# Convolution inputs in a second buffer pool, two narrower operands, and the bias shifts placed one by one in a streaming-encoder layer

## The chip, the cores and the metric

The kernel runs on one core of a Trainium2 chip. The metric is the device time of one execution in microseconds (us), lower is better; a version's time is the median of several runs. One execution is also recorded by the hardware profiler, and all rows of a profile or trace below are from that one.

## The reference: what is computed

One layer of a causal encoder on an input `x` of 2048 tokens by 1024 features, in float32. The input is normalised, multiplied by one wide projection, and the columns of the result feed three groups of heads: chunked softmax attention with a learned bias by relative distance, an mLSTM with a short causal convolution on its queries and keys, and gated linear attention (GLA). The groups are concatenated, projected back and normalised. The parts that the change touches, cut from the reference:

```python
def causal_conv(x, w):                       # 4 taps along the sequence
    xp = jnp.pad(x, ((0, 0), (k_w - 1, 0), (0, 0)))
    return sum(xp[:, j:j + s] * w[j] for j in range(k_w))

z = jnp.einsum('bsd,de->bse', rmsnorm(x, norm_g), w_in)
(aq, ak, av, ag, mq, mk, mv, mo, mi, mf, mg, gq, gk, gv, ga, gg) = jnp.split(z, split_idx, axis=-1)
# attention: scores + bias[clip(relative distance)]; softmax; p @ v; times silu(ag)
qk = jax.nn.silu(causal_conv(jnp.concatenate([mq, mk], axis=-1), conv_w))
# mLSTM on qk, mv with gates mi, mf; times sigmoid(mo), head norm, silu(mg)
log_alpha = jax.nn.log_sigmoid(einsum(ga, w_alpha) + b_alpha) / 16
# GLA on gq, gk, gv with log_alpha; head norm; times silu(gg)
```

## The kernel before, in words

The sequence is cut into four quarters of 512 tokens, `q` = 0 to 3. A first part of the program (call it part A) goes through the quarters: for each it projects the quarter's normalised input onto all columns, and weaves the mLSTM and GLA recurrences in between. Its results go to DRAM. A second part (part B, from `L955` on) reads them back, does the attention and the output projection.

Every projection of 128 columns (`proj_g`, `L231` to `L242`) is 24 matmuls of 128x512: eight blocks of the contraction, each in three products, because both operands are split in a high and a low half. They accumulate in a PSUM bank with the tag `ip`, of which there are two. So a projection can start only when the result of the last but one has been copied out of its bank. That copy is done by ScalarE, mostly: `L547` for the convolution inputs, `L486` (a tanh) for the gate columns, `L513` to `L515` for the values in `evac0`.

**The order of the work.** TensorE's instructions are in the order in which the program issues them (`tc.manual_schedule` names TensorE alone); a small planner, `Flow`, with a hand-written cost per piece, says where the pieces of the recurrences come between the projections. The instructions of all other engines and the DMA issues on the SyncE (SP) queue are ordered by the framework when the program is built, from priorities (the program's order, with the evacuations raised by `AHEAD`) and a simulated timeline. Each engine then runs its list strictly in order: an instruction that waits holds up all behind it. Buffers are taken from pools by name: a tile `name="u", bufs=1` has one buffer, and its next user waits until all readers of the last one are done.

One quarter of part A runs: `proj_z` (GLA's q and k), `proj_v` (values, `proj_t`), `proj_gg`, then `proj_m`, then `proj_gm`, then `proj_a`.

- `proj_m` (`L540` to `L561`) makes six projections, `b` = 0 to 5, the queries and keys of the mLSTM. Each result is copied by ScalarE (`L547`) into `zb`, a tile `u` of 3 + 512 columns with one buffer. GpSimd puts the last three columns of the quarter before in front (`L551`) and saves this one's (`L552`); ScalarE makes the first tap (`L554`), VectorE the other three (`L556`), and a tanh (`L558`, into one of two tiles `e`) and a product (`L559`) finish the SiLU.
- `proj_gm` (`L563` to `L570`) makes six more, `mo0 mg0 mo1 mg1 mo2 mg2`; each is copied out by a tanh in `sig_tile`.
- `gates` is a chain on the few gate columns; its temporaries, and the diagonal matrix `dg` of `prep_x`, the row scale `rbs` and the gate columns `g1` of `prep`, come from a pool `gpool` of five buffers of 512 columns, through `g_tile`.
- `gsel` is a constant matrix: 128 columns that make the GLA decay, then 64 of which the rows 0 to 5 and 32 to 37 of the product are used (`L434` to `L438`).
- `Kt` (7 x 128 columns) holds seven scaled key operands of a GLA chunk; GpSimd writes their first 16 to 112 columns (`L831`), TensorE reads 64 columns of the first four and 128 of the others (`L839`).
- `bias_rel`, called once in the quarter `q` = 1 after `proj_m`, loads the bias table `bt` (128 x 6 x 256) and shifts each head's part by a constant with six ScalarE instructions (`L615`); GpSimd then masks a corner (`L616`). Only part B reads `bt` (`L1071`).

Of the kernel before, what the change touches and what calls it, by code (L numbers as in the profile page):

```python
# [8 lines left out]
FP32 = mybir.dt.float32  # L9
FR = mybir.dt.float32r  # L10
AF = mybir.ActivationFunctionType
# [5 lines left out]
P = 128  # L17
D = 1024
KT = D // P
QT = 512  # L20
# [81 lines left out]
def trunk_kernel(ctx: ExitStack, tc: tile.TileContext, xT, x, w_f, w_t, w_o, w_gates, norm_g, conv_w,  # L102
                 gate_sel, one_row, bias, ml_g, gla_g, final_g, out):
    nc = tc.nc
# [13 lines left out]
    bt = const.tile([P, AH, 256], FP32, name="bt")  # L118
# [24 lines left out]
    with ExitStack() as pa_:  # L143
# [18 lines left out]
        wg = one.tile([P, KT, 32], FP32, name="wg")  # L162
        nc.gpsimd.memset(wg, 0.0)
        onerow = one.tile([P, 1], FP32, name="onerow")
        gsel = one.tile([P, P + 64], FP32, name="gsel")
        zero6 = one.tile([P, 1], FP32, name="zero6")[G0:G0 + MH]
        nc.vector.memset(zero6, 0.0)
        mlg = one.tile([P, 3], FP32, name="mlg")
# [22 lines left out]
            for r in range(4):  # L191
                nc.vector.memset(hs4[32 * h:32 * h + 32, r, 4 * h + r:4 * h + r + 1], 1.0)
        glg = one.tile([P, 2], FP32, name="glg")
        Kt = one.tile([P, 7, P], FP32, name="Kt")
        nc.gpsimd.memset(Kt, 0.0)
        Qb = one.tile([P, 8, 4, 16], FP32, name="Qb")
        nc.gpsimd.memset(Qb, 0.0)
        NP = 4
# [2 lines left out]
        st = {"zb": None, "m": zero6, "S": None, "B": None}  # L201

        def g_tile(shape):
            return gpool.tile(shape, FP32, name="g")

        def load_consts():
            nc.sync.dma_start(cw, conv_w)
# [35 lines left out]
        def proj_f(name, X):  # L243
            out_ = []
            for _ in proj_g(name, X, out_, 4):
                flow.piece(12 * 0.227)
            return out_[0]
# [183 lines left out]
        def gates(q, g1, R):  # L431
            t0 = q * QT
            pb = bank("pw")
            nc.tensor.matmul(pb[0:64], gsel[:, P:P + 64], g1, start=True, stop=True)  # L434
            gi = g_tile([P, QT])[G0:G0 + MH]
            fm = g_tile([P, QT])[G0:G0 + MH]
            nc.vector.tensor_copy(gi, pb[32:32 + MH])
            nc.scalar.copy(fm, pb[0:MH])  # L438
            yield 0.9, 3.0
            pa = bank("pw")  # L440
            nc.tensor.matmul(pa, gsel[:, 0:P], g1, start=True, stop=True)
            ls = big.tile([P, QT], FP32, name="ls", bufs=1)
            log_sigmoid([(ls, pa, g_tile([P, QT])), (fm, fm, g_tile([P, QT])[G0:G0 + MH])])
            R["ls"] = ls
            mr = g_tile([P, QT])[G0:G0 + MH]
            nc.vector.tensor_tensor_scan(mr, fm, gi, st["m"], op0=ALU.add, op1=ALU.max)
            bc = g_tile([P, QT])[G0:G0 + MH]
            for c in range(NC):
                cs = slice(c * L, (c + 1) * L)
                nc.vector.tensor_tensor_scan(bc[:, cs], ones[G0:G0 + MH], fm[:, cs], 0.0, op0=ALU.mult, op1=ALU.add)  # L450
            c4 = lambda t: t.rearrange("p (c t) -> p c t", t=L)
            nm = bc
            gb_ = gi
            nc.vector.tensor_tensor(gb_, gi, bc, op=ALU.subtract)
            nc.scalar.copy(rows[0:MH], gb_)
            nc.scalar.activation(rows[64:64 + MH], mr, AF.Exp, scale=-1.0)
            nc.vector.tensor_tensor(nm, bc, mr, op=ALU.subtract)
            nc.sync.dma_start(nm_d[q], nm)
            nc.vector.tensor_tensor(c4(gb_), c4(gb_), c4(nm)[:, :, L - 1:L].broadcast_to([MH, NC, L]), op=ALU.add)
            nc.scalar.activation(rows[32:32 + MH], gb_, AF.Exp)  # L460
            iw = rows[G0:G0 + MH]
            nc.vector.tensor_tensor(iw[:, 0:L], nm[:, 0:L], st["m"].broadcast_to([MH, L]), op=ALU.add)
            nc.vector.tensor_tensor(c4(iw)[:, 1:NC], c4(nm)[:, 1:NC], c4(mr)[:, 0:NC - 1, L - 1:L].broadcast_to([MH, NC - 1, L]),
                                    op=ALU.add)
            nc.scalar.activation(iw, iw, AF.Exp)
            ml = big.tile([P, 1], FP32, name="ml")[G0:G0 + MH]
            nc.vector.tensor_copy(ml, mr[:, QT - 1:QT])
            st["m"] = ml
            il = iw.rearrange("p (c t) -> p c t", t=L)[:, :, L - 1]
            nc.sync.dma_start(il_d[q], il)  # L470
            iwl = big.tile([P, MH, NC], FP32, name="iwl")
            nc.sync.dma_start(iwl, il_d[q].partition_broadcast(P))
            yield 0.9, 22.0
            rt_ps = bank("pw")
            for c in range(NC):
                nc.tensor.transpose(out=rt_ps[:, c * P:(c + 1) * P], in_=rows[:, c * L:(c + 1) * L], identity=ident)
            rt = big.tile([P, NC, 4, MH], FP32, name="rt")
            nc.vector.tensor_copy(rt, rt_ps.rearrange("p (c r e) -> p c r e", c=NC, r=4)[:, :, :, 0:MH])
            R["rt"] = rt
            R["iwl"] = iwl  # L480
            yield 0.5, 1.0

        def sig_tile(ps):
            th = ev.tile([P, QT], FP32, name="e")
            with tc.high_priority(offset=AHEAD):
                nc.scalar.activation(th, ps, AF.Tanh, scale=0.5)  # L486
            return th

        def silu_tile(ps):
# [50 lines left out]
        def proj_m(X):  # L540
            qk = big.tile([P, 6, QT], FP32, name="qk", bufs=1)
            tail = big.tile([P, 6, 3], FP32, name="tail")
            for b in range(6):
                ps = proj_f(("mq" if b < 3 else "mk") + str(b % 3), X)
                zb = big.tile([P, 3 + QT], FP32, name="u", bufs=1)
                with tc.high_priority(offset=AHEAD):
                    nc.scalar.copy(zb[:, 3:], ps)  # L547
                if st["zb"] is None:
                    nc.gpsimd.memset(zb[:, 0:3], 0.0)
                else:  # L550
                    nc.gpsimd.tensor_copy(zb[:, 0:3], st["zb"][:, b, :])  # L551
                nc.gpsimd.tensor_copy(tail[:, b, :], zb[:, QT:QT + 3])  # L552
                acc = qk[:, b, :]
                nc.scalar.activation(acc, zb[:, 0:QT], AF.Copy, scale=cw[:, b, 0:1])  # L554
                for i in range(1, 4):
                    nc.vector.scalar_tensor_tensor(acc, zb[:, i:i + QT], cw[:, b, i:i + 1], acc, op0=ALU.mult, op1=ALU.add)  # L556
                th = ev.tile([P, QT], FP32, name="e")
                nc.scalar.activation(th, acc, AF.Tanh, scale=0.5)  # L558
                nc.vector.scalar_tensor_tensor(acc, th, 1.0, acc, op0=ALU.add, op1=ALU.mult)  # L559
            st["zb"] = tail  # L560
            return qk  # L561

        def proj_gm(X):  # L563
            gm = big.tile([P, 3, QT], FP32, name="gm", bufs=1)
            for a in range(3):
                th = sig_tile(proj_f(f"mo{a}", X))
                nc.gpsimd.tensor_scalar(th, th, 1.0, mlg[:, a:a + 1], op0=ALU.add, op1=ALU.mult)
                sl = silu_tile(proj_f(f"mg{a}", X))
                nc.gpsimd.tensor_tensor(gm[:, a, :], th, sl, op=ALU.mult)
            return gm  # L570

        def att_in(q, X, b, ps):
# [36 lines left out]
        def bias_rel():  # L609
            bc = big.tile([P, AH], FP32, name="sm")  # L610
            nc.sync.dma_start(bc, bias[:, :, 256])
            nc.scalar.activation(bc, bc, AF.Copy, scale=-1.0)
            nc.sync.dma_start(bt, bias[:, :, 0:256])
            for h in range(AH):
                nc.scalar.activation(bt[:, h, :], bt[:, h, :], AF.Identity, bias=bc[:, h:h + 1])  # L615
            nc.gpsimd.memset(bt[0:64, :, 192:256], NEG)  # L616

        def m_tile(shape):
            return big.tile(shape, FP32, name="m", bufs=3)
# [191 lines left out]
        def gla(q, vg, gg, G, held=None):  # L811
            for sub in range(2):
# [7 lines left out]
                for c in range(2):  # L820
# [7 lines left out]
                        r = slice(32 * h, 32 * h + 32)  # L828
                        nc.scalar.copy(Qb[r][:, :, h, :], b16(qt)[r, 8 * c:8 * c + 8, :])
                    for i in range(1, 8):  # L830
                        nc.gpsimd.tensor_tensor(Kt[:, i - 1, 0:16 * i].rearrange("p (b j) -> p b j", j=16), ko[:, c, 0:i, :],  # L831
                                                Dt[:, c, i, 1:1 + i].unsqueeze(2).broadcast_to([P, i, 16]), op=ALU.mult)
                    tb = bank("gb")
                    nc.tensor.transpose(out=tb[:, 0:P], in_=dr[:, cs], identity=ident)
# [1 line left out]
                    of_ps = bank("ga")  # L836
                    for i in range(1, 8):
                        w = 64 if i < 5 else P
                        nc.tensor.matmul(of_ps[0:w, 64 * i:64 * i + 64], Kt[:, i - 1, 0:w], Qb[:, i, :, :].rearrange("p h i -> p (h i)"),  # L839
                                         start=True, stop=True)  # L840
                    kdt = big.tile([P, P], FP32, name="kdt", bufs=1)
                    nc.scalar.copy(kdt, tb[:, P:2 * P])
# [61 lines left out]
        for q in range(NQ):  # L904
# [32 lines left out]
            qk = proj_m(X)  # L937
            dg = prep_x(q + 1)
            flow.need("gates")
            if q == 1:  # L940
                bias_rel()
            M = dict(R)
            flow.start("mlstm", mlstm(q, qk, vs, M))
            M["gm"] = proj_gm(X)
            R = {}
            flow.start("prep", prep(q + 1, R, dg))
            proj_a(q, X)
# [7 lines left out]
    with ExitStack() as pb_:  # L955
# [3 lines left out]
        one = early  # L959
# [311 lines left out]
def _layout(inputs):  # L1271
# [32 lines left out]
    o["w_gates"] = np.ascontiguousarray(cat("ga", "mi", "mf").reshape(KT, P, 28).transpose(1, 0, 2))  # L1304
    o["norm_g"] = np.ascontiguousarray(a["norm_g"][0].reshape(KT, P).T)
    o["conv_w"] = np.ascontiguousarray(a["conv_w"][0].reshape(4, 6, P).transpose(2, 1, 0))
    gs = np.zeros((4, 32, P + 64), np.float32)
    gs[:, 0:16, 0:P] = a["w_alpha"][0]
    for h in range(MH):
        gs[:, 22 + h, P + 3 * (h % 2) + h // 2] = 1.0  # L1310
# [1 line left out]
    gs[0, 28, 0:P] = a["b_alpha"][0]  # L1312
    gs[0, 28, P:P + MH] = a["b_gates"][0][MH:][[0, 2, 4, 1, 3, 5]]
    gs[0, 28, P + 32:P + 32 + MH] = a["b_gates"][0][:MH][[0, 2, 4, 1, 3, 5]]
    gs = gs.reshape(P, P + 64)
    o["one_row"] = np.zeros((P, 1), np.float32)
    o["one_row"][28] = 1.0
    o["gate_sel"] = gs
# [27 lines left out]
```

## Time and profile before

| | |
|---|---|
| runs | 1284.54, 1284.47, 1280.35 us; median 1284.47 us |
| the profiled execution, device time | 1278.8 us |
| its span, first to last instruction | 1276.9 us |
| outside the span | 1.9 us |
| instructions | TensorE 6804 matmuls, VectorE 1869, ScalarE 1097, GpSimd 761 |
| mean granted TensorE clock | 0.990 |

How to read the rows: PE is a matmul on TensorE, PEld its weight load, DVE is VectorE, ACT is ScalarE, POOL is GpSimd, SP is SyncE, which issues DMAs. `L547` is line 547 of the kernel. A row of a timeline has the start, the duration, the engine, the line, the operation, what it writes and reads, how many were merged, and in brackets how long the engine had been idle and what ended that. A row of a list of waits has who waited for whom, the total in us, how often, and the longest. A row of a table by stretch has the stretch, its length, the busy time of PE, PEld, DVE, ACT and POOL with the count of instructions, the granted clock, the DMA share and GB/s. A row for one line or tile has the durations in ns as lowest/median/highest and the first and last start. Matmuls overlap: the duration of one is longer than the distance from its start to the next one's start.

### The profile page before, as it was taken

The numbers are of one execution on the slowest core, as the hardware profiler recorded it, in microseconds if no ns is written. First come the engines' busy times: TensorE is split into PE (matmuls) and PEld (weight loads), VectorE is DVE, ScalarE is ACT, GpSimd is POOL, SyncE is SP. The second block draws the span as 40 slices with busy tenths as digits, with TensorE's granted clock in tenths as the row PEclk, the third lists the DMA queues.
The fourth block names the chain that finished last, engine by engine and source line by source line (L and its number), as shares of the span: only waits on it lengthen the run. The fifth ranks groups of instructions, "written<-read, shape, count | busy, mean of one in ns | idle before, by whom it ended". The sixth has DMA issues, their size and how long they took to land.

```text
span 1276.9 us, 19361 instructions
## 1 busy us (share of the span) xinstructions
PE 1243.8 (97%) x6804; PEld 1008.3 (79%) x6804; DVE 813.7 (64%) x1869; ACT 590.1 (46%) x1097; POOL 592.2 (46%) x761
## 2 busy tenths in 40 slices
PE   9999999999999999999999999999989999999997
PEld 7777777778777788877778877887867888878886
DVE  6647736772675878266577766675577677666641
ACT  5635432562533346254333643332576565655631
POOL 3336663233666232276622446642364454454442
PEclk7999999999999999999999999999999999999999
DMA  7157344324733442472344233526886456555122
GB/s 246 27 158 259 111 124 150 118 73 131 258 96 114 143 129 66 136 260 88 108 138 124 84 127 98 138 72 175 282 258 205 156 181 207 165 184 172 50 83 82
DMA packets 100185, 184.31 MB, mean 144 GB/s; under 512 B 10592, under 2 KB 46304, under 8 KB 100088
## 3 DMA queue, kind: packets, MB, share of 16 engines
q1 hardware_dynamic: 95624, 174.95, 43.6%
q10 hardware_dynamic: 4464, 8.13, 1.7%
q8 instruction: 53, 0.87, 0.3%
q14 instruction: 44, 0.36, 0.1%
HBM read 147.35 MB, written 35.70 MB: 143 GB/s over the span
## 4 chain that ended last, share of the span: by engine, by line
PE 77%; DVE 8%; POOL 4%; DMA 4%; issue 3%; ACT 3%; SPq 0%; POOLq 0%; DVEq 0%; ACTq 0%
PE ip L236 11%; PE ip L238 10%; PE ip L237 10%; PE ip L256 4%; PE ip L1196 4%; PE ip L1198 4%; PE ip L1197 4%; PE ip L258 4%; PE ip L257 4%; PE s L1055 4%; PE tp L1115 3%; DVE qk L556 2%; PE w L1134 2%; PE ga L839 2%; PE w L1131 2%
## 5 line engine op out<-in xcount | busy, mean ns | idle before, releaser
L236 PE MATMUL ip<-x,w 128*128 128x512 f32 x784 | 318.8, 407 | 3.0 <-ACT u L547 2.7
L238 PE MATMUL ip<-x,w 128*128 128x512 f32 x784 | 306.4, 391 | 0.0
L237 PE MATMUL ip<-x,w 128*128 128x512 f32 x784 | 306.0, 390 | 0.0
L236 PEld LDWEIGHTS ip<-x,w 128*128 128x128 f32 x784 | 147.3, 188 | 46.8 <-issue 12.5
L238 PEld LDWEIGHTS ip<-x,w 128*128 128x128 f32 x784 | 147.2, 188 | 32.4
L237 PEld LDWEIGHTS ip<-x,w 128*128 128x128 f32 x784 | 147.5, 188 | 28.1 <-issue 1.4
L227 ACT CAST w<-wraw 128x1024 fp32r<-128x1024 f32 x126 | 131.7, 1046 | 31.4 <-PE ip L258 10.3
L228 POOL TENSOR_TENSOR w<-wraw,w 128x1024 fp32r<-128x1024 f32 x42 | 100.8, 2401 | 97.0 <-ACT w L227 97.0
L228 DVE TENSOR_TENSOR w<-wraw,w 128x1024 fp32r<-128x1024 f32 x84 | 114.6, 1366 | 45.5 <-ACT w L227 45.4
L1076 POOL TENSOR_SCALAR pt<-pt,sm 128x640 f32<-128x640 f32 (+2 forms) x96 | 72.2, 754 | 118.9 <-DVE sm L1075 92.5
L256 PE MATMUL ip<-w,x 128*128 128x512 f32 x256 | 102.2, 399 | 4.4 <-DVE e L492 2.9
L258 PE MATMUL ip<-w,x 128*128 128x512 f32 x256 | 99.8, 390 | 0.0
L257 PE MATMUL ip<-w,x 128*128 128x512 f32 x256 | 99.7, 390 | 0.0
L781 POOL TENSOR_TENSOR prd<-gk,zg 128x16 f32<-128x16 f32 (+7 forms) x112 | 67.1, 599 | 68.0 <-PE pw L787 62.0
L1074 ACT ACTIVATE pt<-pt,sm 128x640 f32<-128x640 f32 (+2 forms) x96 | 73.3, 763 | 48.3 <-DVE sm L1071 43.9
L1122 DVE TENSOR_TENSOR pl<-tp,ph 128x512 fp32r<-128x512 f32 (+1 forms) x108 | 71.9, 672 | 35.0 <-ACT ph L1121 34.8
L1055 PE MATMUL s<-kk,qq 128*128 128x256 f32 (+2 forms) x360 | 82.4, 314 | 2.3 <-DVE sm L1071 2.2
L778 POOL TENSOR_TENSOR gk<-gk,al 128x16 f32<-128x16 f32 (+14 forms) x120 | 69.6, 580 | 22.1 <-ACT al L755 14.6
L1121 ACT CAST ph<-tp 128x512 fp32r<-128x512 f32 (+1 forms) x108 | 60.3, 572 | 39.7 <-PE tp L1115 37.3
L486 ACT ACTIVATE e<-ip 128x512 f32<-128x512 f32 x44 | 26.2, 595 | 107.5 <-PE ip L238 91.5
L1055 PEld LDWEIGHTS s<-kk,qq 128*128 128x128 f32 x360 | 62.8, 190 | 16.1 <-DVE sm L1071 5.8
L556 DVE SCALAR_TENSOR_TENSOR qk<-u,cw,qk 128x512 f32<-128x512 f32 x72 | 65.7, 913 | 13.7 <-ACT qk L554 12.2
(342 smaller groups left out, 2483.4 us busy)
## 6 DMA issues: line engine op xcount, KB each, us to landing
wraw<-in_w_f SPq DMA_DIRECT2D x100, 512.0 KB, 3.6
wraw<-in_w_t SPq DMA_DIRECT2D x28, 512.0 KB, 3.6
qq<-q_d SPq DMA_DIRECT2D x48, 256.0 KB, 4.8
kk<-k_d SPq DMA_DIRECT2D x18, 512.0 KB, 6.5
vv<-v_d SPq DMA_DIRECT2D x18, 512.0 KB, 5.8
xraw<-in_xT SPq DMA_DIRECT2D x16, 512.0 KB, 8.5
xr<-in_x SPq DMA_DIRECT2D x16, 512.0 KB, 3.7
out<-xr ACTq DMA_DIRECT2D x31, 256.0 KB, 2.2
```

The costliest lines, as they stand in the source:

```text
L227: nc.scalar.copy(w[:, :, 0, :], rv)
L228: other().tensor_tensor(w[:, :, 1, :], rv, f32(w[:, :, 0, :]), op=ALU.subtract)
L236: nc.tensor.matmul(ps, w[:, k, 0, :], X[k][:, 0, :], start=(k == 0), stop=False)
L237: nc.tensor.matmul(ps, w[:, k, 0, :], X[k][:, 1, :], start=False, stop=False)
L238: nc.tensor.matmul(ps, w[:, k, 1, :], X[k][:, 0, :], start=False, stop=(k == KT - 1))
L256: nc.tensor.matmul(ps, X[k][:, 0, t], w[:, 0, :], start=(k == 0), stop=False)
L257: nc.tensor.matmul(ps, X[k][:, 0, t], w[:, 1, :], start=False, stop=False)
L258: nc.tensor.matmul(ps, X[k][:, 1, t], w[:, 0, :], start=False, stop=(k == KT - 1))
L556: nc.vector.scalar_tensor_tensor(acc, zb[:, i:i + QT], cw[:, b, i:i + 1], acc, op0=ALU.mult, op1=ALU.add)
L1055: nc.tensor.matmul(sp[:, :cn], qq[:, l, tt * P:(tt + 1) * P], kk[:, ko + c0:ko + c0 + cn], start=(l == 0), stop=(l == 1))
L1074: nc.scalar.activation(pt[:, :n], pt[:, :n], AF.Exp, bias=init, scale=-1.0, accum_out=sm[:, 2:3])
L1076: nc.gpsimd.tensor_scalar(pt[:, :n], pt[:, :n], sm[:, 3:4], 0.5, op0=ALU.mult, op1=ALU.mult)
```

## The change

Four edits.

1. `g_tile` makes every buffer of `gpool` three columns wider and hands out its first 512 columns. In `proj_m` the odd inputs (`b` = 1, 3, 5) take their `zb` from `gpool`; the even ones stay in the single `u`.
2. `gsel` loses its last 16 columns, 64 becomes 48.
3. `Kt` becomes two tiles: four operands of 64 columns and three of 128.
4. `bias_rel` becomes a generator. Its loads stay where they were; each of the six shifts is issued in `proj_gm` of the quarter 1 after one of the six tanhs, and tied behind that tanh in ScalarE's list with `tc.issue_after`; the mask follows the last.

```diff
-        gsel = one.tile([P, P + 64], FP32, name="gsel")
+        gsel = one.tile([P, P + 48], FP32, name="gsel")
...
-        Kt = one.tile([P, 7, P], FP32, name="Kt")
-        nc.gpsimd.memset(Kt, 0.0)
+        Kh = one.tile([P, 4, 64], FP32, name="Kh")
+        nc.gpsimd.memset(Kh, 0.0)
+        Kl = one.tile([P, 3, P], FP32, name="Kt")
+        nc.gpsimd.memset(Kl, 0.0)
+        Kt = [Kh[:, i] for i in range(4)] + [Kl[:, i] for i in range(3)]
...
         def g_tile(shape):
-            return gpool.tile(shape, FP32, name="g")
+            t = gpool.tile([P, 3 + QT], FP32, name="g")[:, 0:QT]
+            return t.rearrange("p (c t) -> p c t", c=shape[1]) if len(shape) > 2 else t
...
-            nc.tensor.matmul(pb[0:64], gsel[:, P:P + 64], g1, start=True, stop=True)
+            nc.tensor.matmul(pb[0:48], gsel[:, P:P + 48], g1, start=True, stop=True)
...
-                nc.scalar.activation(th, ps, AF.Tanh, scale=0.5)
+                st["th"] = nc.scalar.activation(th, ps, AF.Tanh, scale=0.5).ins
...
-                zb = big.tile([P, 3 + QT], FP32, name="u", bufs=1)
+                zb = gpool.tile([P, 3 + QT], FP32, name="g") if b % 2 else big.tile([P, 3 + QT], FP32, name="u", bufs=1)
...
-        def proj_gm(X):
+        def proj_gm(X, shift=None):
             gm = big.tile([P, 3, QT], FP32, name="gm", bufs=1)
             for a in range(3):
                 th = sig_tile(proj_f(f"mo{a}", X))
+                if shift:
+                    next(shift)
                 nc.gpsimd.tensor_scalar(th, th, 1.0, mlg[:, a:a + 1], op0=ALU.add, op1=ALU.mult)
                 sl = silu_tile(proj_f(f"mg{a}", X))
                 nc.gpsimd.tensor_tensor(gm[:, a, :], th, sl, op=ALU.mult)
+                if shift:
+                    next(shift)
...
             for h in range(AH):
-                nc.scalar.activation(bt[:, h, :], bt[:, h, :], AF.Identity, bias=bc[:, h:h + 1])
+                yield
+                with tc.issue_after(st["th"]):
+                    nc.scalar.activation(bt[:, h, :], bt[:, h, :], AF.Identity, bias=bc[:, h:h + 1])
             nc.gpsimd.memset(bt[0:64, :, 192:256], NEG)
+            yield
...
-                        nc.gpsimd.tensor_tensor(Kt[:, i - 1, 0:16 * i].rearrange("p (b j) -> p b j", j=16), ko[:, c, 0:i, :],
+                        nc.gpsimd.tensor_tensor(Kt[i - 1][:, 0:16 * i].rearrange("p (b j) -> p b j", j=16), ko[:, c, 0:i, :],
...
-                        nc.tensor.matmul(of_ps[0:w, 64 * i:64 * i + 64], Kt[:, i - 1, 0:w], Qb[:, i, :, :].rearrange("p h i -> p (h i)"),
+                        nc.tensor.matmul(of_ps[0:w, 64 * i:64 * i + 64], Kt[i - 1], Qb[:, i, :, :].rearrange("p h i -> p (h i)"),
...
-            if q == 1:
-                bias_rel()
+            shift = bias_rel() if q == 1 else None
+            if shift:
+                next(shift)
...
-            M["gm"] = proj_gm(X)
+            M["gm"] = proj_gm(X, shift)
```

The packed constant in DRAM has 48 columns there as well.

More of the change, by code (lines that the diff above doesn't have):

```diff
@@ L1306, in _layout @@
     o["conv_w"] = np.ascontiguousarray(a["conv_w"][0].reshape(4, 6, P).transpose(2, 1, 0))
-    gs = np.zeros((4, 32, P + 64), np.float32)
+    gs = np.zeros((4, 32, P + 48), np.float32)
     gs[:, 0:16, 0:P] = a["w_alpha"][0]
@@ L1314, in _layout @@
     gs[0, 28, P + 32:P + 32 + MH] = a["b_gates"][0][:MH][[0, 2, 4, 1, 3, 5]]
-    gs = gs.reshape(P, P + 64)
+    gs = gs.reshape(P, P + 48)
     o["one_row"] = np.zeros((P, 1), np.float32)
```

## The prediction

> **What bounds the kernel now.** I read the page's busy times first, then TensorE's own waits, then the timelines of the engines around each wait that the change touches.
>
> ```profile
> span 1276.9 us, 19361 instructions
> PE 1243.8 (97%) x6804; PEld 1008.3 (79%) x6804; DVE 813.7 (64%) x1869; ACT 590.1 (46%) x1097; POOL 592.2 (46%) x761
> ```
>
> TensorE works for 1243.8 of 1276.9 us, so 33.1 us are all that any edit beside its matmuls can win. The change removes no matmul and leaves the order of TensorE's list as it is: that list is the program's own, and the planner's costs aren't edited. So the question is which TensorE waits go and which come.
>
> ```profile
> PE w L1131 <- ACT ph L1121: 3.8, 3, 2.3
> PE w L1134 <- DVE pl L1122: 3.7, 6, 2.1
> PE ip L256 <- DVE e L492: 2.9, 1, 2.9
> PE ip L236 <- ACT u L547: 2.7, 2, 2.5
> ...
> PE ip L256 <- ACT vg L515: 1.4, 1, 1.4
> ```
>
> In this list of TensorE's waits two rows belong to the change. The 2.7 us on L547 are projections that find no free bank because the copy into `u` is late. The 1.4 us on L515 are a value copy; what it was late behind is below. The top two rows lie in part B.
>
> **Odd convolution inputs in the pool.** The longer of the two L547 waits, seen on TensorE, ScalarE, VectorE and GpSimd:
>
> ```profile
> 566.68 0.39 PE L237 MATMUL ip<-x,w 128*128 128x512 f32 x1
> 566.91 0.39 PE L238 MATMUL ip<-x,w 128*128 128x512 f32 x1
> 569.83 0.50 PE L236 MATMUL ip<-x,w 128*128 128x512 f32 x1 [2.53 <-ACT u L547]
> ```
> ```profile
> 560.14 0.57 ACT L547 COPY u<-ip 128x512 f32<-128x512 f32 x1
> ...
> 562.79 1.04 ACT L227 CAST w<-wraw 128x1024 fp32r<-128x1024 f32 x1
> 569.19 0.58 ACT L547 COPY u<-ip 128x512 f32<-128x512 f32 x1 [5.36 <-DVE qk L556]
> ```
> ```profile
> 554.48 2.72 DVE L556 SCALAR_TENSOR_TENSOR qk<-u,cw,qk 128x512 f32<-128x512 f32 x3 [1.08 <-ACT qk L554]
> ...
> 562.92 0.75 DVE L556 SCALAR_TENSOR_TENSOR qk<-u,cw,qk 128x512 f32<-128x512 f32 x1 [0.45 <-ACT qk L554]
> 563.63 3.65 DVE L285 TENSOR_SCALAR g<-ident,rs 128x128 f32<-128x128 f32 x4
> 567.20 1.88 DVE L556 SCALAR_TENSOR_TENSOR qk<-u,cw,qk 128x512 f32<-128x512 f32 x2
> ```
> ```profile
> 564.81 2.39 POOL L228 TENSOR_TENSOR w<-wraw,w 128x1024 fp32r<-128x1024 f32 x1
> ```
>
> Matmuls start 566.91 - 566.68 = 0.23 us apart, and the next start came 2.92 us later: 2.69 us lost. ScalarE stood 5.36 us before the copy of the third input, because VectorE was still reading the second one from the single `u`; between the first and the second of its three taps VectorE made the diagonal, 3.65 us of it while GpSimd's split ran. With the change the third input (`b` = 2) takes the `u` of the first, whose taps ended at 554.48 + 2.72 = 557.20. So its copy can run when ScalarE has ended the cast, 562.79 + 1.04 = 563.83, well before the bank was missed at 567.14: the 2.69 us go whole, with 3.3 us to spare. What is late next is the fifth input, which needs the third one's taps: these start when VectorE has ended the second's (569.08) and take about 2.7 us, to 571.8, while the fifth projection, 24 matmuls of 0.23 us after 567.14, ends at 572.7. No wait is left there. The second L547 wait goes too:
>
> ```profile
> 576.32 0.50 PE L236 MATMUL ip<-x,w 128*128 128x512 f32 x1 [0.19 <-ACT u L547]
> ```
>
> That is 0.19 us, together 2.88. In the other three quarters TensorE doesn't wait on L547, so nothing is won there; ScalarE alone gains room:
>
> ```profile
> ACT e L558 <- DVE qk L556: 29.5, 10, 4.3
> ...
> ACT u L547 <- DVE qk L556: 19.9, 8, 5.4
> ```
>
> Can the pool run short? It has five buffers. The gate chain's own temporaries are done long before `proj_m`; what can stand beside three inputs is `dg`:
>
> ```profile
> L285 DVE TENSOR_SCALAR g<-ident,rs x12: 273/594/2430, 112.8 to 564.9; 128x128 f32<-128x128 f32 x12
> ...
> L293 PE MATMUL pw<-g,ones x6: 592/594/595, 188.7 to 641.8; 128*128 128x512 f32 x6
> ```
>
> It is written from 112.8 and read at 188.7 us, across the end of `proj_m`: 3 + 1 of 5 buffers, no wait, cost 0. VectorE, which now decides when the inputs come free, isn't full in that stretch, 32.64 of 46 us:
>
> ```profile
> 548.00:594.00 46.00, 43.28 (x225) 34.03 (x224) 32.64 (x42) 25.37 (x43) 33.26 (x48) 1.00 0.56 204
> ```
>
> The diagonal took up to 2430 ns beside its lowest of 273, with GpSimd's split running. The Trainium skill (page "SBUF — State Buffer", on the shared port pair) has a rule for this that speaks against a full gain: a VectorE instruction in a two-port mode, or one with two SBUF inputs, is blocked whole by a GpSimd instruction that reads SBUF and began first. A second buffer shortens no tap, so by the rule the chain stays as late as it was, and at worst the convolution's part of the sum is 0 in place of 2.88; the row agrees with the block, not yet with that end.
>
> **Bias shifts.** ScalarE in the second quarter's `proj_v`:
>
> ```profile
> 271.11 2.50 ACT L615 ACTIVATE bt<-bt,sm 128x256 f32<-128x256 f32 x6
> 273.52 0.47 ACT L513 ACTIVATE v<-ip 128x384 f32<-128x384 f32 x1
> 273.89 0.24 ACT L515 COPY vg<-ip 128x128 f32<-128x128 f32 x1
> ```
> ```profile
> 272.40 0.39 PE L258 MATMUL ip<-w,x 128*128 128x512 f32 x1
> 274.19 0.50 PE L256 MATMUL ip<-w,x 128*128 128x512 f32 x1 [1.40 <-ACT vg L515]
> ```
>
> The six shifts run in one piece, the two copies that free a bank stand behind them, and TensorE loses 274.19 - 272.40 - 0.23 = 1.56 us. After the change each shift, 2.50 / 6 = 0.42 us, stands behind a tanh of `proj_gm`, 100 us later, where ScalarE has room:
>
> ```profile
> 370.00:410.00 40.00, 40.00 (x243) 32.10 (x242) 23.18 (x50) 12.31 (x20) 28.97 (x42) 1.00 0.32 100
> ...
> 370.20 0.60 ACT L486 ACTIVATE e<-ip 128x512 f32<-128x512 f32 x1 [1.91 <-PE ip L238]
> 377.67 0.60 ACT L486 ACTIVATE e<-ip 128x512 f32<-128x512 f32 x1 [5.94 <-POOL prd L781]
> ```
>
> It works 12.31 of 40 us there. A shift delays what is behind it by 0.42 us, and the next copy isn't due for a whole projection, 5.5 us: cost 0; without that cover 6 x 0.42 = 2.5 us. The mask, once on GpSimd, waits for the last shift; behind it are GpSimd's GLA products, which have this stage's slack. The small constant now holds one of two `sm` buffers for longer, while one mLSTM chunk at a time uses the other. The table's load stays where it is in the program. Gain 1.56 us.
>
> **The narrow operands.**
>
> ```profile
> L434 PE MATMUL pw<-g,gsel x8: 592/618/643, 36.6 to 700.6; 128*64 128x512 f32 x8
> ...
> L441 PE MATMUL pw<-g,gsel x8: 591/592/595, 43.2 to 705.8; 128*128 128x512 f32 x8
> ```
>
> 64 columns of weights are no faster than 128, so 48 are put at 0 (8 rows, at most 8 x 0.03 = 0.2 us either way). The key operands are read in the same widths as before. One memset of 896 columns at the start becomes two of 256 and 384; GpSimd waits there later anyway: 0. In bytes, 64 + 1024 per partition come free and 5 x 12 are taken.
>
> **The sum.** 2.88 + 1.56 = 4.44 us, and 0 to 0.4 us of cost: 4.4 us. The profiled execution would be 1278.8 - 4.4 = 1274.4. The median of the runs is 1284.47, 5.7 us above that execution, and the runs themselves spread over 4.2 us (1280.35 to 1284.54). About 0.5%, 6.4 us, is what a measurement of this kernel can tell from no change. I put the same gain on the median: **1280.1 us**.
>
> What no row shows is the new order on ScalarE, VectorE, GpSimd and SP: it is made from a simulated timeline, in which these buffers come free at other times. It can move waits anywhere behind the first `proj_m`, down to part B, whose tiles also lie over part A's at shifted addresses. Its bounds are the largest cluster of waits in the trace, at the start of part B:
>
> ```profile
> 936.00:957.00 21.00, 14.97 (x86) 11.73 (x84) 16.20 (x42) 15.74 (x36) 16.38 (x15) 0.95 1.03 303
> ...
> 950.00:960.00 10.00, 5.55 (x22) 4.14 (x22) 7.03 (x10) 5.98 (x12) 6.45 (x4) 0.74 0.98 303
> 956.00:966.00 10.00, 7.97 (x37) 6.34 (x38) 8.94 (x24) 5.40 (x13) 4.63 (x5) 0.72 0.65 236
> ```
>
> TensorE is idle for 21.00 - 14.97 = 6.0 us of the first stretch, and after that the granted clock falls to 0.72 for 10 us, about 2.8 us more: 8.8 us in one place that could go either way.
>
> **The rivals.**
>
> *The convolution's wait comes back.* ScalarE's new list puts the tanh L558, which waits for the same taps, ahead of the third copy; or VectorE's chain falls a projection further behind. For: 29.5 us of L558 waits. Against: the copies have raised priority. Then only the bias part is won: 1284.47 - 1.6 = 1282.9 us. The same would follow if the shifts were bunched again and the convolution alone won, 1281.6.
>
> *Better than the sum.* The new order thins the cluster at 936 to 957, or the waits fall so that the clock stays up. Half to all of 8.8 us on top: 1280.1 - 4.4 to 1280.1 - 8.8, 1275.7 to 1271.3 us. For: the two largest rows of TensorE's waits are there. Against: nothing in the change aims at it.
>
> *Slower: a load of output weights slips on the SP queue.*
>
> ```profile
> 920.94 7.84 SPq L576 DMA_DIRECT2D ga_d<-e  x2
> ...
> 951.77 1.14 ACT L1022 CAST x<-xr 128x512 fp32r<-128x512 f32 x2 [2.60 <-DMA xr<-in_w_o]
> ```
>
> ScalarE already waits 2.60 us for these weights, with casts for TensorE behind it, so the load has no slack: each us that its issue comes later is a us on TensorE. Pieces of SP's list stand for up to 7.84 us before it. If the new order puts one such piece ahead of the load, that costs 7.8 us and about 2.8 more of low clock: 1280.1 + 10.6 = 1290.7 us. It decides from a slip of 4.4 us on; from there the gain is eaten. Against: part A keeps its program order, and the load belongs to part B.
>
> **How the numbers follow.** The forecast has 0.50, the returned wait 0.14, better than the sum 0.24, the slipped load 0.12. By the run's spread, the forecast itself reaches from 1275.9 to 1280.1 and a little above. Faster means under 1278.0: 0.21 of the better case and 0.10 of the forecast, 0.31. Slower means over 1290.9: 0.07, the further half of the slipped load. The rest, 0.62, is the same. The range 1272.5 to 1287.0 leaves out the end of the better case and most of the slipped load, under 2 in 10.
>
> **What would show it.** Right: no TensorE wait on L547 in the third quarter; the third copy near 563 us there; the six shifts single, each behind an L486 from about 365 to 405 us; no wait at 272; the start of part B some 4.4 us earlier and unchanged in itself. Wrong: an L547 or L486 wait in any `proj_m`; a wait on a pool buffer; a stretch around 930 to 965 with another idle sum or clock.

## The result, and the profile after

| | before | after |
|---|---|---|
| median of 6 runs each | 1282.43 us | 1274.79 us |
| lowest and highest | 1279.36 to 1285.72 | 1272.83 to 1275.66 |
| profiled execution, span | 1276.9 | 1271.1 |

The ratio of the times is 0.9941, with an interval of 0.9927 to 0.9955: 7.6 us faster, 0.6%. A second set of runs gave 0.9948 (0.9929 to 0.9968). Lines of the changed kernel stand 4 to 12 further down than before: `L547` is `L551`, `L787` is `L798`, `L1121` in part B is `L1133`.

The page of the changed kernel, its span and busy times:

```profile
span 1271.1 us, 19322 instructions
PE 1239.6 (98%) x6804; PEld 1006.4 (79%) x6804; DVE 815.6 (64%) x1869; ACT 590.1 (46%) x1097; POOL 597.4 (47%) x762
```

The matmuls are the same 6804. TensorE is busy 4.2 us less than before, ScalarE as long, VectorE 1.9 and GpSimd 5.2 us more; GpSimd has one instruction more, the second memset. TensorE's list of waits in the changed kernel (who waited for whom, total us, times, longest):

```profile
PE w L1143 <- ACT ph L1133: 4.8, 3, 3.2
PE w L1146 <- DVE pl L1134: 3.7, 7, 1.9
PE ip L260 <- DVE e L496: 2.9, 1, 2.9
...
PE pw L798 <- POOL prd L792: 1.5, 1, 1.5
PE ga L360 <- DVE vg L358: 1.5, 2, 1.0
...
PE ip L240 <- ACT vg L519: 0.2, 1, 0.2
```

Both rows that the change was to remove are gone: no wait on the copy of a convolution input (`L551`), no wait of 1.4 us on the value copy. A new row stands there, 1.5 us on GpSimd's products `prd`. The row on `vg` was 0.5 us before; what it has gained lies in the first 7 us of the span, and it is 0.6 us in the second profile of the changed kernel. Of part B's rows the one on `ph` is 1.0 us longer, the others nearly as they were.

At the place of the wait behind the bias shifts the matmuls now start 0.22 us apart:

```profile
269.49 0.39 PE L262 MATMUL ip<-w,x 128*128 128x512 f32 x1
269.71 0.39 PE L260 MATMUL ip<-w,x 128*128 128x512 f32 x1
```

As TensorE's list is the same in both programs, each matmul can be set beside its twin, and the difference of their starts followed along the span. It moves in few places. The places are times of the trace of before, a minus is earlier, and a step is the difference between the median shift of ten neighbouring starts behind the place and ahead of it.

| at, us | what | step, us |
|---|---|---|
| up to 40 | start of the span, granted clock | -2.4 |
| 130, 355 | transpose behind the GLA copy `dr` | -0.4, -0.5 |
| 274 | value copy behind the bias shifts | -1.7 |
| 365 | GLA matmul behind the product `at` | -0.9 |
| 570 | copy of the third convolution input | -2.8 |
| 576 | GpSimd's products, less the second wait on an input copy | +1.9 |
| 783 | value projection behind the product `e` | -0.4 |
| part B, 895 to 985 | waits and clock | +2.1 |

The steps listed add up to -5.2, and a slow drift between them to -0.6, together the -5.8 of the spans. What belongs to the change as such, without the start and part B, is -4.9 us in steps and -0.7 of drift, -5.6 us. At the start the program is the same but for the memsets, and the granted clock was not: from 18 to 26 us it was 0.69 of the full clock before and 1.00 after, and 2.0 of the 2.4 us lie there. In both kernels' tables by stretch (stretch, length, busy PE, PEld, DVE, ACT, POOL, clock), before first:

```profile
0.00:30.00 30.00, 27.10 (x126) 22.64 (x126) 20.16 (x56) 15.50 (x18) 11.72 (x24) 0.77 0.75 262
```
```profile
0.00:30.00 30.00, 25.88 (x136) 21.38 (x137) 20.51 (x57) 16.31 (x20) 11.59 (x25) 0.89 0.73 262
```

0.77 against 0.89 of the full clock, in one execution each. So the spans of two profiles of this kernel cannot be subtracted to the microsecond. Single steps in part A are steadier: the one at 274 us is -1.7 in all eight profiles of kernels with the shifts moved and at most 0.1 in the other three, the one at 570 us is -2.8 in all seven with the odd inputs in the pool.

The experiments below give another measure beside the ratio: the span of each run, less the clock time lost in it (span times one less the mean granted clock), as a mean over the runs. I call it the remainder. Among 32 runs of the kernel before, spans and lost clock time go together with a correlation of 0.84; the ten with a clock of 0.989 had a mean span of 1280.5 us, the six with 0.992 one of 1277.9. The clock of one run is given to 0.001, 1.3 us of a span; by the spread of the runs a set's remainder is good to 0.2 to 0.9 us (standard error). In the runs of before one us of lost clock time went with 0.7 to 0.8 us of span, so where the lost times of two sets differ, the remainder takes off a little too much.

The third quarter after the change, on ScalarE:

```profile
550.02 0.57 ACT L551 COPY g<-ip 128x512 f32<-128x512 f32 x1
...
555.61 0.56 ACT L551 COPY u<-ip 128x512 f32<-128x512 f32 x1
...
562.96 0.63 ACT L562 ACTIVATE e<-qk 128x512 f32<-128x512 f32 x1 [4.69 <-DVE qk L560]
563.50 0.57 ACT L551 COPY g<-ip 128x512 f32<-128x512 f32 x1
```

The second input goes to `g` at 550.02 where it went to `u` at 560.14, and the third follows at 555.61, 13.6 us earlier than before (6.2 of them are the shift of all that came before). ScalarE still stands for VectorE's taps, 4.69 us, now for a tanh with the fourth input's copy behind it, but by then no bank is missed. Now the matmuls in front of the bank that was missed:

```profile
566.13 0.39 PE L242 MATMUL ip<-x,w 128*128 128x512 f32 x1
566.44 0.61 PE L798 MATMUL pw<-prd,hs 128*32 128x208 f32 x6
568.59 0.62 PE L798 MATMUL pw<-prd,hs 128*32 128x256 f32 x2 [1.53 <-POOL prd L792]
569.13 0.50 PE L240 MATMUL ip<-x,w 128*128 128x512 f32 x1
```

The projection's last matmul is followed at once, but the next piece in TensorE's fixed order is a group of eight GLA matmuls, and the last two need a product that GpSimd hadn't made. It was in TensorE's list before, too, behind the wait for the bank, which hid it.

### The profile page after: what moved, and what is told of

It is laid out like the page before. It is cut to its first block, busy times and chain, and to the rows that moved or that the text cites. A ratio compares the mean times of both kernels' runs of the same rounds, so it can differ in the third digit from the quotient of the medians.

```text
span 1271.1 us, 19322 instructions
## 1 busy us (share of the span) xinstructions
PE 1239.6 (98%) x6804; PEld 1006.4 (79%) x6804; DVE 815.6 (64%) x1869; ACT 590.1 (46%) x1097; POOL 597.4 (47%) x762
## 4 chain that ended last, share of the span: by engine, by line
PE 89%; DVE 3%; DMA 2%; issue 2%; POOL 2%; ACT 1%; SPq 0%; POOLq 0%; DVEq 0%; ACTq 0%
PE ip L240 14%; PE ip L241 13%; PE ip L242 13%; PE ip L260 4%; PE ip L262 4%; PE ip L261 4%; PE ip L1208 4%; PE ip L1210 4%; PE ip L1209 4%; PE s L1067 4%; PE tp L1127 3%; PE ga L850 2%; PE w L1146 2%; PE w L1143 2%; PE s L704 2%
## 5 line engine op out<-in xcount | busy, mean ns | idle before, releaser
L1133 ACT CAST ph<-tp 128x512 fp32r<-128x512 f32 (+1 forms) x108 | 60.4, 572 | 41.3 <-PE tp L1127 38.5
L1127 PE MATMUL tp<-ident,pt 128*128 128x128 f32 x420 | 62.5, 274 | 2.5 <-POOL pt L1088 2.5
```

The costliest lines, as they stand in the source:

```text
L1127: nc.tensor.transpose(out=tp[:, w + x_ * P:w + (x_ + 1) * P], in_=pt[:, (b - b0) * P:(b - b0 + 1) * P], identity=ident)
```

## The experiments

Each ratio is to runs of the kernel before made beside it on the same chip, with its interval. There were three such sets of the kernel before, with remainders of 1266.9, 1266.4 and 1266.6 us; each difference below is to the one of its own set, unless another is named.

### The convolution inputs and the narrow operands alone

The changed kernel with the bias shifts as before:

```diff
-            shift = bias_rel() if q == 1 else None
-            if shift:
-                next(shift)
+            if q == 1:
+                bias_rel()
...
-            M["gm"] = proj_gm(X, shift)
+            M["gm"] = proj_gm(X)
```

> Odd convolution inputs in the wider pool and the narrow operands, the bias shifts left in one piece. If the parts add up as the waits in the two traces say, this gives the convolution's steps alone: TensorE's wait on the input copy in the third quarter goes (2.7 us), the three short waits of the GLA stages behind the input copies go (2.0 us), the new wait on GpSimd's products may stay (1.9 us back), and the 1.4 us wait on the value copy behind the bias shifts stays: 3 to 5 us faster than before. If instead the new order of the other engines' lists as a whole makes the difference, it is anything from 0 to 8 us faster, and part B's start changes by itself.

Ratio 0.9965 (0.9952 to 0.9979), median 1276.99 us; remainder 1262.5, 4.4 us under. TensorE's waits:

```profile
PE pw L791 <- POOL prd L785: 1.7, 1, 1.7
PE ip L260 <- ACT vg L519: 1.4, 1, 1.4
```

The wait behind the bias shifts stays, that on the copies is gone, that on GpSimd's products is there: the first theory, within its 3 to 5 us. The small steps are there too: -0.4 at 130 us, -0.5 at 355, -0.9 at 365, -0.4 at 783. In its profile part B takes 5.2 us longer than in that of before, which is the sign that the second theory names; why it does not decide stands below, with the rivals of the prediction.

### The bias shifts alone, twice

The kernel before with `bias_rel`, `proj_gm` and the calls as in the change, all else untouched.

> The bias shifts spread over the gate projections alone; buffers and operands as before. If the parts add up: the wait of 1.4 us on the value copy in the second quarter goes, the waits on the convolution input's copy stay (2.7 us in the third quarter), 1.6 to 1.8 us faster. If the new order makes the difference, 0 or over 4 us. If the shifts cost what they save in the new place, 0, with waits of TensorE on the tanhs of the gate projections.

Ratio 0.9999 (0.9982 to 1.0016), median 1281.95 us, and yet the wait is gone, and a longer one is left alone:

```profile
PE ip L256 <- DVE e L492: 2.7, 1, 2.7
...
PE ip L236 <- ACT u L547: 2.5, 1, 2.5
```

No row on the value copy of over 0.2 us is left. Matmul by matmul the step at 274 us is -1.7. The remainder is 1264.8, 2.1 us under, while the lost clock time was 14.7 us against 13.3. The time alone says no gain, the other two say the forecast's. So it was run again:

> The bias shifts spread alone, once more, since the first time the median did not move though the span less the lost clock time fell by 2.1 us. Theory: the waits removed are worth 1.8 us, so the span less the lost clock time is again 1.5 to 2.5 us under that of before, and the ratio of the times is about 0.9985 over both sets, with the rest the chance of low-clock windows. Rival: with the wait gone TensorE falls into a low-clock window more often, the lost clock time is again 1 us or more above that of before, and the ratio stays at 1.000.

Ratio 0.9981 (0.9966 to 0.9995), median 1280.10 us; remainder 1264.2, 2.4 us under; lost clock time 14.0 against 13.9. The step at 274 us is -1.7 again. The rival, that the clock takes the gain back, falls. The two ratios' intervals overlap around 0.999, and a gain of 1.7 us in 1282 is 0.9987.

### The narrow operands alone

The kernel before with `gsel` of 128 and 48 columns in place of 128 and 64, and with `Kt` as two tiles.

> The two narrow operands alone. Theory: 48 columns of weights take what 64 take, and the key operands are read in the widths as before, so 0 within 0.2 us of work, no TensorE wait comes or goes, and the time is that of before within 1.5 us. Rival: the shifted addresses or the split key tile change the order of the lists or the releases at the start of part B, and 1 to 3 us of the gain belong to them.

Ratio 0.9990 (0.9973 to 1.0007), remainder 1266.4, 0.5 us under: nothing that can be measured. In its profile the longest wait on `dr` is 1.1 us where before had 0.2, and the one on the input copy 1.9 where before had 2.5. The second profile of the shifts alone, without these edits, has the same 1.1 and 1.9, so they are not the operands'. In the changed kernel the small matmul, now with 48 columns, takes 592/612/630 ns, where 64 took 592/618/643:

```profile
L438 PE MATMUL pw<-g,gsel x8: 592/612/630, 34.3 to 693.2; 128*48 128x512 f32 x8
```

### The shifts in one piece in the new place

The changed kernel, all six shifts behind the first tanh of `proj_gm`:

```diff
-            for h in range(AH):
-                yield
+            yield
+            for h in range(AH):
                 with tc.issue_after(st["th"]):
...
-                if shift:
+                if shift and a == 0:
                     next(shift)
...
-                if shift:
-                    next(shift)
             return gm
```

> The whole change, but the six bias shifts stand in one piece behind the first tanh of the gate projections instead of one behind each tanh. Theory: the piece is 2.5 us, the next copy out of a bank is due 5.5 us after the tanh and a bank is missed only 5.5 us after that, so the place is what matters and not the spreading: the time of the changed kernel within 1 us, no TensorE wait in that stage. Rival: the spreading matters, 1 to 2.5 us slower than the changed kernel, with a TensorE wait behind a tanh near 365 us.

Ratio 0.9957 (0.9944 to 0.9970), median 1276.36 us; remainder 1260.6, where the changed kernel had 1260.3 in its first six runs and 1261.5 in the next seven. ScalarE in that stage:

```profile
361.49 0.58 ACT L490 ACTIVATE e<-ip 128x512 f32<-128x512 f32 x1
361.97 2.49 ACT L623 ACTIVATE bt<-bt,sm 128x256 f32<-128x256 f32 x6
364.36 0.36 ACT L895 ACTIVATE n<-ga 128x256 f32<-128x256 f32 x1
366.48 0.60 ACT L490 ACTIVATE e<-ip 128x512 f32<-128x512 f32 x1 [1.76 <-PE ip L242]
```

After 2.49 us of shifts ScalarE is idle for 1.76 us before the next tanh, and TensorE has no wait between 360 and 410 us. The median is 1.6 us above the changed kernel's first, more than the 1 us expected. The intervals overlap, the remainders agree within their errors, and these runs lost 14.0 us of clock time where the changed kernel lost 12.5 and 12.0, which is as much as the medians differ. So the place is what removed the wait; that spreading adds anything is not shown.

### The changed kernel once more

> The changed kernel once more, to have its runs and clocks beside those of the others. Theory: the span less the clock time lost to the low clock (span times one less the mean granted clock) is about 6.5 us under that of the kernel before, the sum of the convolution part (4.4 us so measured) and the bias part (2.1 us), and what the medians differ from that is the chance of low-clock windows. Rival: the parts do not add up, and the difference so measured is 4.4 us or less, or over 8 us.

Ratio 0.9948, median 1275.37 us; remainder 1261.5, 4.8 us under, not the 6.5 expected. In its profile what belongs to the change is -5.1 us, drift included, the wait on GpSimd's products being longer:

```profile
569.81 0.62 PE L798 MATMUL pw<-prd,hs 128*32 128x256 f32 x2 [2.18 <-POOL prd L792]
```

Over both sets, 13 runs, the remainder is 1261.0, some 5.7 us under the mean of the three of before, with a standard error of 0.6.

### All six inputs from the pool

```diff
-                zb = gpool.tile([P, 3 + QT], FP32, name="g") if b % 2 else big.tile([P, 3 + QT], FP32, name="u", bufs=1)
+                zb = gpool.tile([P, 3 + QT], FP32, name="g")
```

> The whole change with all six convolution inputs from the pool of five, not the odd ones alone. Theory: in the changed kernel no TensorE wait on an input copy is left, so nothing is to be won; the time of the changed kernel within 1 us, and with the diagonal at most five buffers are wanted at once. Rival: the pool runs short, and the copies wait for the diagonal or the third input before: 1 to 3 us slower, with a TensorE wait on a copy into the pool.

Ratio 0.9944 (0.9924 to 0.9964), remainder 1260.6: the changed kernel's time. The waits on the input copies in ScalarE's list are all for TensorE:

```profile
ACT g L551 <- PE ip L242: 19.5, 10, 4.2
```

So the pool's five buffers are enough for all six inputs beside the diagonal, and the odd inputs alone already gave all there was to win.

### The small copies on ScalarE

The changed kernel, with the head and the tail of each convolution input copied by ScalarE:

```diff
-                    nc.gpsimd.tensor_copy(zb[:, 0:3], st["zb"][:, b, :])
-                nc.gpsimd.tensor_copy(tail[:, b, :], zb[:, QT:QT + 3])
+                    nc.scalar.copy(zb[:, 0:3], st["zb"][:, b, :])
+                nc.scalar.copy(tail[:, b, :], zb[:, QT:QT + 3])
```

> The whole change with the small copies of three columns (the head of each convolution input and the saved tail) on ScalarE, not GpSimd. Theory: the new TensorE wait of 1.5 us on GpSimd's products in the third quarter is GpSimd held by these copies and its split, so it shrinks or goes, 1 to 1.9 us faster than the changed kernel. Rival: GpSimd is late there by the split and the products alone, the wait stays within 0.5 us, and ScalarE's extra instructions cost 0 to 2 us.

Ratio 0.9942 (0.9920 to 0.9965), median 1275.20 us; remainder 1258.9, 7.5 us under that of before and 2.6 under the changed kernel measured beside it, with a standard error of 1.1. GpSimd in the changed kernel, ahead of the late product, and TensorE's row in this one:

```profile
564.02 0.65 POOL L555 COPY g<-tail 128x3 f32<-128x3 f32 x1
564.63 0.63 POOL L792 TENSOR_TENSOR prd<-gk,zg 128x240 f32<-128x240 f32 x1
565.21 1.18 POOL L556 COPY tail<-g 128x3 f32<-128x3 f32 x1
566.35 1.13 POOL L789 TENSOR_TENSOR gk<-gk,al 128x240 f32<-128x240 f32 x1
567.56 0.97 POOL L792 TENSOR_TENSOR prd<-gk,zg 128x256 f32<-128x256 f32 x1
```
```profile
567.16 0.62 PE L798 MATMUL pw<-prd,hs 128*32 128x256 f32 x2 [0.32 <-POOL prd L792]
```

Two copies of three columns took 0.65 and 1.18 us of GpSimd's time just before the product that TensorE waited for; at their shortest they take 0.18. The second ended 0.05 us behind a VectorE product that ran from 565.05 to 566.34 us; whether that held it up was not tried. Without the copies the wait falls from 1.53 (2.18 in the second profile) to 0.32 us, and TensorE's step there from 1.9 and 2.5 to 0.7 us. The mechanism is shown; in the time it can't be told from the changed kernel (1275.20 against 1275.37 us), as this set lost 14.4 us of clock time against the changed kernel's 12.0.

### The diagonal on ScalarE, in the kernel before

```diff
-                nc.vector.tensor_scalar(dg[:, tt, :], ident, rs[:, tt:tt + 1], None, op0=ALU.mult)
+                nc.scalar.activation(dg[:, tt, :], ident, AF.Copy, scale=rs[:, tt:tt + 1])
```

> The kernel before, with the diagonal made by ScalarE in place of VectorE; single input buffer, bias shifts in one piece. Theory: the long TensorE wait in the third quarter (2.5 us) is the diagonal between two taps, held up by GpSimd's split; without it the taps end some 3.5 us earlier and the wait goes, 2 to 3 us faster than before, while the 1.4 us wait behind the bias shifts stays. Rival: VectorE's taps are late anyway by other instructions, or ScalarE now stands before the row scale; the wait stays at 2 us or more, and the time is that of before.

Ratio 0.9979 (0.9962 to 0.9996), median 1279.78 us, 2.2 us under that of before as the theory had it; remainder 1265.5, only 0.9 under. VectorE and TensorE in the third quarter:

```profile
561.55 2.75 DVE L556 SCALAR_TENSOR_TENSOR qk<-u,cw,qk 128x512 f32<-128x512 f32 x3 [0.44 <-ACT qk L554]
```
```profile
574.05 0.50 PE L236 MATMUL ip<-x,w 128*128 128x512 f32 x1 [1.20 <-ACT u L547]
```

The second input's three taps run through in 2.75 us and the wait for its buffer is gone; the next bank is then missed, by 1.20 us, for the fourth input. So the diagonal on VectorE was the cause of that wait, and with the single buffer the next late copy made a wait as well.

### Both together

The small copies and the diagonal on ScalarE, in the changed kernel.

> The whole change, with the small copies on ScalarE (the TensorE wait on GpSimd's products was 0.3 us with them) and the diagonal on ScalarE too. Theory: GpSimd's wait stays at 0.3 us or goes; span less lost clock time 1 to 3 us under that of the changed kernel. Rival: ScalarE, with 16 more small instructions a quarter, delays copies out of the banks, and the time is that of the changed kernel or 1 us over.

Ratio 0.9940 (0.9920 to 0.9959), median 1273.91 us, remainder 1259.8, 6.9 us under. TensorE's wait on GpSimd is 0.7 us, not the 0.3 or less expected, and the remainder is 1.2 us under the changed kernel's 1261.0 of other sets. It is the lowest median of all, but its interval is that of the changed kernel: a version that beats it is not shown.

## Why the prediction was right, and where it was short

**The time.** 1280.1 was forecast, with 1272.5 to 1287.0 as the range; 1274.79 came out. The forecast said 4.4 us and *no change* as the likeliest; 7.6 us and just over the bound of 0.5% were measured, a case that had 0.31. Of the 5.3 us between forecast and time, 2.0 are the base: three runs of the kernel before gave the 1284.47 that the forecast started from, six gave 1282.43. The other 3.2 are the gain. The time falls between the 1275.7 and 1271.3 of the rival *better than the sum*, but not by its cause: that was a thinner cluster or a better clock at the start of part B, and part B got no faster. So the cause was right, the sum too small, and the case that had 0.24 came out in its number by another way.

**The two waits.** Both went, where and as it was said. The long wait on the copy: 2.69 us forecast, 2.8 us at its place. The shifts: 1.56 us forecast, 1.7 at their place, and 2.1 and 2.4 in the remainders of the shifts alone. The differences are the matmul right behind a wait, from whose start to the next one it took 0.33 us (569.83 to 570.16) and not 0.23.

**"In the other three quarters ... nothing is won there; ScalarE alone gains room."** This is the step that failed: it put the other quarters at nothing. That room was worth 0.4 + 0.5 + 0.9 + 0.4 = 2.2 us in the first, second and fourth quarters. TensorE's list of waits before did name products of ScalarE and VectorE there, in small rows that the prediction left out:

```profile
PE ga L857 <- DVE at L851: 0.6, 1, 0.6
...
PE gb L834 <- ACT dr L791: 0.4, 2, 0.2
```

One of them, before, and the same matmul after:

```profile
364.44 0.39 PE L238 MATMUL ip<-x,w 128*128 128x512 f32 x1
365.44 0.67 PE L857 MATMUL ga<-Sbd,q 128*128 128x256 f32 x2 [0.61 <-DVE at L851]
```
```profile
359.25 0.39 PE L242 MATMUL ip<-x,w 128*128 128x512 f32 x1
359.48 0.59 PE L868 MATMUL ga<-Sbd,q 128*128 128x256 f32 x2
```

From start to start it is 1.00 us before and 0.23 after, though the wait is booked with 0.61. A matmul's record lasts 0.39 us and the next starts 0.23 us after it, so each of these waits costs 0.16 us more than its idle time, and the wait of 0.19 us at 130 us cost 0.35. All seven kernels with the odd inputs in the pool have these steps, the convolution part alone included. The operands alone have 0.0 at 355, 365 and 783 us, and the shifts alone have 0.0 at 365 and 783. So the steps at 365 and 783 us are the convolution inputs': ScalarE, no longer standing before a copy, makes the next casts and copies sooner. The two behind `dr` are less sure. At 130 us the kernels without the pool were 0.2 to 0.9 us later than before, by execution, and at 355 us the shifts alone had -0.1 and -0.5, and the kernel with the diagonal on ScalarE -0.6. The drift of -0.7 us, too, is in all seven and in none of the others; its cause is open. That this is the whole path in each place was read from the timelines, not tried.

**"No wait is left there."** One was: 1.5 to 2.2 us on GpSimd's products. The argument had followed VectorE and ScalarE behind the missed bank, not what TensorE's own list has next. In the sum it took 1.9 to 2.5 us back, net of the second wait on an input copy (0.19 us in the forecast, 0.27 from start to start), which went. With it part A adds up: 2.8 + 1.7 + 2.2 + 0.7 - 1.9 = 5.5, 5.6 before rounding.

**The pool.** No matmul waits for a buffer, as forecast. But GpSimd does, which the prediction named as a sign of error. In the changed kernel:

```profile
256.88 0.64 POOL L555 COPY g<-tail 128x3 f32<-128x3 f32 x1 [13.55 <-DVE g L275]
259.11 0.53 POOL L768 COPY gk<-zg 128x256 f32<-128x256 f32 x1 [1.58 <-ACT zg L533]
```

The new order put the head of the next quarter's first odd input so early that it stood for 13.55 us for a temporary of the gate chain, and twice more in the later quarters, 28.0 us in all. It costs nothing, since GpSimd's next instruction had to wait 1.6 us more for `zg` each time, here to 259.11.

**The cover of the shifts, the operands.** The shifts stand single in `proj_gm`, as forecast:

```profile
L625 ACT ACTIVATE bt<-bt,sm x6: 497/508/511, 359.6 to 396.8; 128x256 f32<-128x256 f32 x6
```

The cost of 0 there held, even for all six in one piece: TensorE has no wait in that stage. The operands show no cost and no gain.

**The rivals.** The returned wait didn't come, and the Trainium skill's rule on the shared port pair (page "SBUF — State Buffer") did not decide here: in the changed kernel a tap took up to 2768 ns, in the third quarter with GpSimd's split running, against a median of 886 on the same buffer, and TensorE didn't wait for one. The slipped load didn't come either: part B lost 2.2 us against before in both profiles, not 10.6, and TensorE's idle time in the stretch at 936 to 957 us stayed at 5.9 against 6.0. That part B became slower is not shown: the profile of before is a quick execution, 1276.9 us where 32 spans have a mean of 1280.2, and the place at 895 to 985 us took 1.2 to 4.4 us longer in all eleven other profiles, that of the operands alone included (1.5).

**What stays open**, beside the drift, is the last 1 to 2 us. The changed kernel's two sets lost 12.5 and 12.0 us of clock time, the kernel before 13.3 to 13.9. That adds to the remainder's 5.7 us and makes about the 6.6 to 7.6 us of the medians. But kernels with the same edits lost 12.7 to 14.4 us, so it may be chance.

## What to carry to other kernels

Where one engine is busy throughout, take its waits from start to start, not from the idle time that is listed, and count the small ones that stand behind the same engine as the big one. A single buffer between two in-order engines cost more here than the one wait that it showed, since what stood behind the waiting copy was late too. When a wait is to go, read what the waiting engine's own list has next, and who makes that.

## What the runs showed of the hardware

Equal programs had mean granted clocks of 0.985 to 0.993 in 32 runs, and their spans went from 1274.9 us (at 0.993) to 1287.3 (at 0.987). With such a spread an effect of 2 us showed in the ratio in one set of the shifts alone (0.9981) and not in the other (0.9999), while the remainder and the matmuls' steps found it in both.
